# A two-layer hybrid encoder layer on one core: projections 512 columns wide, channel-major gates, x fed transposed, transposes issued singly, one weight ring

## The chip, the cores and the metric

The kernel runs on one core of a Trainium2 chip. Its time is the device time of one execution in microseconds (us). The core has five engines that this text names as the profile does: PE (TensorE, matmuls and transposes, with PEld for its weight loads), DVE (VectorE), ACT (ScalarE), POOL (GpSimd) and SP (SyncE), which here only issues the transfers between HBM and the on-chip memory, one after the other, each after the semaphores that it waits for.

## What is computed

One layer over 2048 positions of width 1024, in float32. The input is RMS-normalised and projected to 4616 columns; three groups of heads read the projection; their outputs are joined, projected back and added to the input.

```python
h = rms_norm(x, norm_g[l])
proj = jnp.einsum('bsd,de->bse', h, w_in[l])
(a_q, a_k, a_v, a_z, m_q, m_k, m_v, m_o, m_z, m_i, m_f, c_a, c_b, c_z) = split_columns(proj)
...
att = chunk_band_attention(q, k, v, ...) * jax.nn.silu(a_z)      # 4 heads of 64, own chunk + 8 before
qk = jax.nn.silu(causal_depthwise_conv(concat([m_q, m_k]), ...)) # width 4
hm = mlstm_chunkwise(m_q, m_k, m_v, i_pre, f_pre)                # 4 heads of 128
ml = rms_norm(sigmoid(m_o) * hm, ml_out_g) * jax.nn.silu(m_z)
u = causal_depthwise_conv(c_a * jax.nn.sigmoid(c_b), ...)        # width 31
cv = jax.nn.silu(layer_norm(u, ...)) * jax.nn.silu(c_z)
x = x + jnp.einsum('bse,ed->bsd', concat([att, ml, cv]), w_out[l])
```

## The kernel before

The sequence is worked through in four rounds of 512 positions (`q` in the code, `TQ` = 512), each of four blocks of 128. In each round x is loaded row by row (`x_load`), scaled by its RMS, transposed on PE in tiles of 128x128 and split into two parts, high and low, of the rounded type `fp32r`, so that three matmul passes (high x high, high x low, low x high: `PASS`) stand for one float32 matmul. The two halves of a round's transposed x are the tiles `xT` of 256 positions each.

The projection is cut into 21 units of 256 columns (264 for the one that carries the gates), and the output projection into 4 of them. A unit is computed in one of two ways. `tm` gives positions on the partitions: for a block of 128 positions 8 k-steps of 3 passes, 24 matmuls with a moving operand of 256 weight columns. `cm` gives channels on the partitions: 128 channels, and twice 24 matmuls that move 256 positions each. Keys, queries, values, the gates o and z of each mLSTM head, the gate of the convolution group and the output are `tm`; the inputs of both convolutions and the attention gate are `cm`.

Weights arrive in the first round as float32 (`fetch_w`, tiles `wr`), are split by ACT (high part) and POOL (low part) in `split_w`, are written back to HBM split (`keep`, `wk<-w`) and are loaded split in the later three rounds (`fetch_split`, `w<-wk`). Two pools hold them: 6 tiles `wr`, 10 tiles `w`.

PE's order is the order in which the code calls it. A clock in the code (`clk`, advanced by an assumed price of each matmul) and coroutines (`spawn`, `tick`, `wait_for`) place the work of the attention, the mLSTM heads and the layer norm between the k-steps of the units: a coroutine yields a time from the table `L`, and its next piece is put on PE when the code's clock has passed it. So a transpose or a matmul of a head that needs a result of DVE stands a fixed piece of PE's work behind it; if the result is later than that, PE, which works in order, waits. For head h `do_head` computes the unit with k and q (`cm` twice); `conv_silu` takes each result off PSUM (ACT copy to `mraw`, then on DVE one scaling and three multiply-adds into `macc`, a tanh on ACT, one last multiply on DVE). `head_chain` then transposes k (`pk`), `L["kk"]` = 8.52 after k's unit, multiplies k by q (`pS`), `L["qq"]` = 8.0 after q's unit, and goes through the four blocks (`pp`, three matmuls each). The width-31 convolution is 60 multiply-adds a round on DVE (`cvu`), fed in one by one (`TAP`). The other engines and SP are ordered by the framework's scheduler.

Of the kernel before, what the change touches and what calls it, by code (L numbers as in the profile page):

```python
# [26 lines left out]
U_AK, U_AV, U_AQ, U_AZ, U_CZ = 0, 1, 2, 3, 4  # L27
U_V = (5, 6)
U_QK = (7, 8, 9, 10)
U_OZ = (11, 12, 13, 14)  # L30
U_C = (15, 16)
WB = 10
RB = 6
XB, OB, HB = 6, 6, 6
PTB, QSB, PRB = 2, 1, 3
DEPTH = 3
TAP = 2.21
LNH = 3
L = {"x": 6.51, "xg": 1.4, "k": 11.25, "q": 5.7, "qt": 1.48, "s": 0.32, "t": 1.6, "pv": 0.45, "s0": 4.0,
     "g0": 14.0, "g1": 4.37, "g2": 6.03, "g3": 5.23, "g4": 2.6, "kk": 8.52, "qq": 8.0, "ps": 2.2, "ch": 2.4,  # L40
     "ln": 3.61, "mix": 0.79, "wp": 1.85, "w0": 0.19, "xb": 0.5, "mx1": 1.12, "mx2": 1.39}
U_OUT = (17, 18, 19, 20)
# [3 lines left out]
def kernel(ctx: ExitStack, tc: tile.TileContext, x, wu, wg, norm_g, qg, kg, bias, far,  # L46
# [7 lines left out]
    xpool = ctx.enter_context(tc.tile_pool(name="xpool", bufs=3))  # L54
# [14 lines left out]
    def slot(name, n, dt=F32, tag="H"):  # L69
        return sl.tile([P, n], dt, name=name, tag=tag, bufs={"X": XB, "O": OB, "H": HB}[tag],  # L70
                       padded_shape=[P, 512 if tag == "X" else 516])
# [7 lines left out]
    gx = ctile([P, D], "gx")  # L79
    mask = ctile([P, P], "mask")  # L80
    G.memset(mask, 0.0)
    G.affine_select(out=mask, in_=mask, compare_op=ALU.is_ge, fill=NEG, base=0,
                    pattern=[[1, P]], channel_multiplier=-1)
    mhalf = ctile([P, 16], "mhalf")
    G.memset(mhalf, -0.5)
    zrow = ctile([16, P], "zrow")
    G.memset(zrow, 0.0)

# [7 lines left out]
    mlg = ctile([P, 512], "mlg")  # L96
    cvw_t = ctile([P, 2, CW], "cvw_t")
    cvb_t = ctile([P, 2], "cvb_t")
    lng = ctile([P, 256], "lng")
    lnb = ctile([P, 256], "lnb")  # L100
    wgs = ctile([P, 2, KT, 8], "wgs", F32R)
    wgr = ctile([P, KT, 8], "wgr")

    def load_consts():
        nc.sync.dma_start(out=gqk, in_=qg.partition_broadcast(P))
        nc.sync.dma_start(out=kg_t, in_=kg.partition_broadcast(P))
        V.scalar_tensor_tensor(out=gqk, in0=gqk, scalar=0.125, in1=kg_t, op0=ALU.mult, op1=ALU.mult)
        nc.sync.dma_start(out=bias_t, in_=bias.rearrange("h p k -> p h k"))
        nc.sync.dma_start(out=far_t, in_=far.partition_broadcast(P))
        G.memset(bias_t[0:64, :, 192:256], NEG)  # L110
        nc.sync.dma_start(out=mcw_t, in_=mcw)
# [19 lines left out]
    cvh = ctile([P, 2, CW - 1], "cvh")  # L131
    for h in range(4):
        G.memset(cst[h], 0.0)
    G.memset(mst, 0.0)
    G.memset(mch, 0.0)
    G.memset(cvh, 0.0)

# [854 lines left out]
```

## Time and profile before

| | |
|---|---|
| time, median of 3 runs | 1252.62 us (1251.28 to 1252.7) |
| profiled execution: its time, and its span | 1250.82 us, 1249.0 us |
| busy share of the span: PE, DVE, ACT, POOL | 96%, 65%, 31%, 21% |
| mean granted TensorE clock | 0.996 of full |
| moved by the DMA engines | 235.51 MB, mean 189 GB/s |

The span runs from the first to the last instruction of the profiled execution; what lies around it is 1.8 us. The profile prints busy times, which for PE count a matmul from its start to its modelled end while the next one already runs; so the distance between starts, not the printed mean of one matmul, is what a matmul costs.

### The profile page before, as it was taken

What the parts mean: (1) busy time and instruction counts of PE and PEld (TensorE: products, weight loads), DVE (VectorE), ACT (ScalarE), POOL (GpSimd) and SP (SyncE); (2) the same over time, 40 slices, a digit from 0 to 9 for tenths busy, and PEclk for the clock granted to TensorE, in tenths of its full rate; (3) what the DMA queues carried; (4) which work ended last, traced back from release to release, by engine and by line L of the source; (5) the groups of instructions that cost most, each with busy time, mean ns of one, the idle gap of its engine ahead of it and who ended that gap; (6) DMA issues with size and microseconds to landing.
All of it is one profiled execution on the core that took longest, in us unless ns stands there. A gap on an engine that the chain in (4) does not pass through costs nothing.

```text
span 1249.0 us, 25880 instructions
## 1 busy us (share of the span) xinstructions
PE 1201.4 (96%) x10188; PEld 1177.1 (94%) x10188; DVE 815.0 (65%) x2125; ACT 390.2 (31%) x1023; POOL 262.1 (21%) x312
## 2 busy tenths in 40 slices
PE   6999989889899999999999999999999999999998
PEld 6999889889899999999999999999999999999998
DVE  7368998884316888876431788877632288887641
ACT  5345433333122442223221343222312144322220
POOL 5553444644111000130010100013101010012200
PEclk9999999999899999999999999999999999999999
DMA  9956465668745244454675432555476532345453
GB/s 315 366 205 218 164 226 203 220 220 281 266 167 197 88 134 152 152 189 181 239 238 185 163 110 85 184 189 186 151 248 244 203 138 86 135 162 184 162 179 127
DMA packets 101345, 235.51 MB, mean 189 GB/s; under 512 B 11560, under 2 KB 45160, under 8 KB 101224
## 3 DMA queue, kind: packets, MB, share of 16 engines
q1 hardware_dynamic: 101224, 233.87, 54.2%
q8 instruction: 80, 1.31, 0.4%
q14 instruction: 41, 0.34, 0.1%
HBM read 181.27 MB, written 52.56 MB: 187 GB/s over the span
## 4 chain that ended last, share of the span: by engine, by line
PE 79%; DVE 10%; DMA 5%; issue 3%; POOL 2%; ACT 1%; SPq 0%; POOLq 0%; ACTq 0%; DVEq 0%
PE pmm L155 64%; PE pp L155 3%; PE pss L155 2%; PE po L155 2%; PE ptp L160 2%; DMA dt<-fr 2%; PE ptx L160 2%; DVE macc L634 1%; DMA wk<-w 1%; DVE cvu L726 1%; PE pS L155 1%; POOL w L248 1%; DMA wr<-in_wu 1%; PE ptq L160 1%; DVE dt L648 1%
## 5 line engine op out<-in xcount | busy, mean ns | idle before, releaser
L155 PE MATMUL pmm<-w,xT 128*128 128x256 f32 (+1 forms) x3840 | 516.5, 287 | 6.7 <-DVE xT L266 2.4
L155 PEld LDWEIGHTS pmm<-w,xT 128*128 128x128 f32 x3840 | 476.5, 190 | 12.0 <-issue 2.9
L155 PE MATMUL pmm<-xT,w 128*128 128x256 f32 x2688 | 344.6, 285 | 0.0
L155 PEld LDWEIGHTS pmm<-xT,w 128*128 128x128 f32 x2688 | 327.7, 189 | 2.3 <-issue 1.9
L155 PE MATMUL pmm<-w,mT 128*128 128x256 f32 x1536 | 198.0, 286 | 8.1 <-DVE xr L914 6.5
L155 PEld LDWEIGHTS pmm<-w,mT 128*128 128x128 f32 x1536 | 187.8, 191 | 9.6 <-DVE xr L914 6.9
L726 DVE SCALAR_TENSOR_TENSOR cvu<-cvu,cvw_t 128x512 f32<-128x512 f32 x240 | 184.3, 768 | 0.9
L248 POOL TENSOR_TENSOR w<-wr,w 128x512 fp32r<-128x512 f32 x80 | 110.9, 1397 | 117.6 <-ACT w L208 104.1
L621 POOL TENSOR_TENSOR gz<-gz,mlg 128x512 f32<-128x512 f32 x16 | 23.8, 1486 | 326.0 <-DVE gz L618 266.1
L914 DVE TENSOR_TENSOR xr<-pmm,xr 128x256 f32<-128x256 f32 x64 | 27.0, 423 | 91.8 <-PE pmm L155 75.3
L634 DVE SCALAR_TENSOR_TENSOR macc<-mraw,mcw_t,macc 128x512 f32<-128x512 f32 x96 | 75.6, 787 | 1.0
L720 DVE SCALAR_TENSOR_TENSOR cvu<-cvt,pmm 128x512 f32<-128x512 f32 x8 | 5.5, 690 | 102.5 <-PE pmm L155 102.5
L208 ACT ACTIVATE pr<-pr,nm 128x640 f32<-128x640 f32 (+4 forms) x64 | 49.1, 767 | 45.1 <-DVE nm L463 45.0
L208 ACT CAST w<-wr 128x512 fp32r<-128x512 f32 x82 | 49.2, 616 | 8.2 <-issue 4.0
L208 ACT ACTIVATE kw<-og 128x128 f32<-128x128 f32 x64 | 19.8, 310 | 99.3 <-DVE og L689 91.9
L208 ACT CAST xT<-ptx 128x512 fp32r<-128x512 f32 x32 | 18.8, 587 | 99.8 <-PE ptx L160 99.7
L208 ACT COPY pT<-ptp 128x384 f32<-128x384 f32 (+2 forms) x64 | 29.5, 461 | 59.3 <-PE ptp L160 59.3
L155 PE MATMUL pss<-kT,qT 128*128 128x320 f32 (+4 forms) x224 | 44.6, 315 | 2.8 <-DVE nm L463 2.8
L681 DVE SCALAR_TENSOR_TENSOR cst<-cst,dec,pp 128x129 f32<-128x129 f32 x64 | 22.2, 348 | 33.9 <-PE pp L155 33.5
L208 ACT ACTIVATE og<-pmm 128x128 f32<-128x128 f32 x64 | 17.5, 274 | 81.8 <-PE pmm L155 81.7
L160 PE MATMUL ptp<-ident_r,pr 128*128 128x128 f32 x280 | 41.8, 273 | 0.0
L155 PE MATMUL po<-pT,vR 128*64 128x128 f32 x560 | 38.9, 279 | 0.6 <-DVE pT L487 0.5
(251 smaller groups left out, 1384.3 us busy)
## 6 DMA issues: line engine op xcount, KB each, us to landing
w<-wk SPq DMA_DIRECT2D x240, 512.0 KB, 5.2
wk<-w SPq DMA_DIRECT2D x80, 512.0 KB, 5.3
wr<-in_wu SPq DMA_DIRECT2D x84, 256.0 KB, 4.7
xs<-in_x SPq DMA_DIRECT2D x16, 512.0 KB, 6.2
xr<-in_x SPq DMA_DIRECT2D x64, 128.0 KB, 2.7
out<-xr SPq DMA_DIRECT2D x64, 128.0 KB, 4.6
w<-wk SPq DMA_DIRECT2D x12, 528.0 KB, 5.5
dt<-fr SPq DMA_DIRECT2D x16, 256.0 KB, 3.3
```

The source lines that it names most:

```text
L155: last[0] = tc.keep_in_program_order(PE.matmul(out_, lhsT=lhsT, rhs=rhs, start=start, stop=stop))
L160: tc.keep_in_program_order(PE.transpose(out=out_, in_=in_, identity=(ident_r if rnd else ident)[0:n, 0:n]))
L208: i = fn(*a, **k)
L248: lo = G.tensor_tensor(out=w[:, 1, :, 0:256], in0=raws[g], in1=f(w[:, 0, :, 0:256]), op=ALU.subtract)
L621: G.tensor_tensor(out=gz, in0=gz, in1=mlg[:, h * P:(h + 1) * P].unsqueeze(1).to_broadcast([P, NB, P]), op=ALU.mult)
L634: V.scalar_tensor_tensor(out=acc, in0=raw[:, j:j + 512], scalar=mcw_t[:, i, j:j + 1], in1=acc, op0=ALU.mult, op1=ALU.add)
L648: V.scalar_tensor_tensor(out=dt[:, b, :], in0=dt[:, b, :], scalar=cols[:, 0, h, b:b + 1], in1=mask, op0=ALU.add, op1=ALU.min)
L681: V.scalar_tensor_tensor(out=cst[h], in0=cst[h], scalar=dec[:, h * NB + b:h * NB + b + 1], in1=pu[:, 0:129], op0=ALU.mult, op1=ALU.add)
L720: V.scalar_tensor_tensor(out=u[:, CW - 1:CW + 511], in0=t, scalar=1.0, in1=pa, op0=ALU.add, op1=ALU.mult)
L726: queue_after(V.scalar_tensor_tensor(out=acc, in0=u[:, i:i + 512], scalar=cvw_t[:, j, i:i + 1], in1=acc, op0=ALU.mult, op1=ALU.add), last[0])
L914: V.tensor_tensor(out=xr, in0=ps[:, 0:256], in1=xr, op=ALU.add)
```

## The change

- Every unit is 512 wide. `tm` now moves 512 weight columns (k and v of the attention in one unit, all of m_v, all of m_o), `cm` moves all 512 positions of the round. The query unit with the gates stays at 264.
- The gates z of the mLSTM heads, the gate of the convolution group and the output projection are computed with channels on the partitions (`cm`). The norms of the heads' outputs (`og`, scaled on ACT) and of the convolution group are transposed after normalising (`pto`, `pty`) and gated there; the per-channel factors (`mlg`, `lng`, `lnb`) become per-partition scalars. The output is written transposed, and turned on the host.
- x is also passed in transposed (`xT` in HBM), and x's transposes on PE go. The rows of x are still read for the sums of squares; the row factors reach the transposed x by a matmul of ones with a diagonal (`spread`, `prs`). `x_first` does this for the first round block by block, `x_next` for a later round during the output projection.
- In a coroutine `yield FINE` puts each transpose behind one matmul (`sip`), where four stood together.
- One ring of 12 tiles (`WB`) holds both unsplit weights (two pieces in a tile) and split ones. Weights are handled in 84 pieces; a `tm` unit uses 8 of them (4 for the queries) in each block and frees them in the last, a `cm` unit uses 2.
- `conv_silu`: the scaling is done by ACT from PSUM, the small copies by POOL; there is one buffer for `mraw` (tag "M") and two for `macc` (tag "A", shared with x's tiles `xk`), where both came from a pool of 6. A head's units are put on PE only after the head before has taken its q (`"taken"`).
- The order of the units and the constants `L`, `TAP` are new.

```diff
-WB = 10
-RB = 6
-XB, OB, HB = 6, 6, 6
+WB = 12
+LAG = 5
+XB, HB, AB, MB = 5, 4, 2, 1
...
-     "g0": 14.0, "g1": 4.37, "g2": 6.03, "g3": 5.23, "g4": 2.6, "kk": 8.52, "qq": 8.0, "ps": 2.2, "ch": 2.4,
+     "g0": 15.0, "g1": 4.8, "g2": 6.0, "g3": 5.7, "g4": 2.8, "kk": 9.3, "qq": 8.8, "ps": 2.4, "ch": 2.6,
...
+FIRST = ["kv", "cb0", "ca0", "cb1", "ca1", "qg", "v", "mk0", "mq0", "o"]
+LATER = ["cb0", "ca0", "kv", "cb1", "ca1", "qg", "v", "mk0", "mq0", "o"]
...
-        clk["t"] += max(n, 256) / 2400.0 if lhsT.dtype == F32R else 4.0 * n / 2400.0
+        clk["t"] += 0.006 + 0.00044 * n if lhsT.dtype == F32R else share * 2 * (0.003 + n / 1200.0)
...
+    def sip():
+        for c in chains:
+            if c["fine"]:
+                step(c)
+                return
...
+    def new_w(i, j):
+        flat = wpool.tile([P, 1056], F32R, name=f"w_{i}", tag="w", bufs=WB)
+        ring.append(lambda: j < st["used"] and (j >= NPIECE or i in kept))
+        return flat[:, 0:2 * cols(i)].rearrange("p (a c) -> p a c", a=2)
...
+    def keep(i, w):
+        kept[i] = dram.tile([P, 2, cols(i)], F32R, name=f"wk_{i}", tag=f"wk_{i}")
+        nc.sync.dma_start(out=f(kept[i]), in_=f(w))
...
-    def tm(xts, wt, b, n=256):
-        for k in range(KT):
-            for s_, m_ in PASS:
-                mm(ps[:, 0:n], xt[:, s_, k, c], wt[k // 2][:, m_, k % 2, 0:n], i == 0, i == 3 * KT - 1)
+    def tm(xt, u, b):
+        for k in range(KT):
+            w = piece((st["used"] if b == NB - 1 else j0 + k // step_))
+            for s_, m_ in PASS:
+                mm(ps[:, 0:n], xt[:, s_, k, c], w[:, m_, :], i == 0, i == 3 * KT - 1)
+                sip()
...
-    def cm(xts, wt, c0):
-        for p in range(2):
-            for k in range(KT):
-                for s_, m_ in PASS:
-                    mm(ps[:, p * 256:(p + 1) * 256], wt[k // 2][:, s_, k % 2, c0:c0 + P], xts[p][:, m_, k, :],
-                       i == 0, i == 3 * KT - 1)
+    def cm(xt, u):
+        for k in range(KT):
+            w = piece(st["used"]).rearrange("p a (k c) -> p a k c", k=4)
+            for s_, m_ in PASS:
+                mm(ps, w[:, s_, k % 4, :], xt[:, m_, k, :], i == 0, i == 3 * KT - 1)
+                sip()
...
+    def x_first(xt):
+        for b in range(NB):
+            t = io.tile([P, D], F32, name="xs", tag="io", padded_shape=[P, 1056])
+            nc.sync.dma_start(out=t, in_=x[b * P:(b + 1) * P, :])
+            xtb = raw[:, b * D:(b + 1) * D].rearrange("p (k t) -> p k t", k=KT)
+            nc.sync.dma_start(out=xtb, in_=xT[:, b * P:(b + 1) * P].rearrange("(k p) t -> p k t", p=P))
...
+            dg = spread(rs, [b])
+            mm(pr[:, 0, :], ones, dg[:, 0, :], True, True)
...
+    def x_next(q, xt, lnc):
+        while not lnc["done"]:
+            yield 0.5
...
+        for k in range(KT):
+            xk = slot("xk", 512, tag="A")
+            nc.sync.dma_start(out=xk, in_=xT[k * P:(k + 1) * P, q * TQ:(q + 1) * TQ])
+            if k:
+                finish_x(xt, k - 1, prev, rb)
...
-    def conv_silu(q, ps, i):
-        raw = slot("mraw", 516)
-        V.tensor_copy(out=raw[:, 0:3], in_=mch[:, i, :])
+    def conv_silu(ps, i):
+        raw = slot("mraw", 516, tag="M")
+        G.tensor_copy(out=raw[:, 0:3], in_=mch[:, i, :])
         A.copy(out=raw[:, 3:515], in_=ps)
-        acc = slot("macc", 512)
-        V.tensor_scalar(out=acc, in0=raw[:, 3:515], scalar1=mcw_t[:, i, 3:4], scalar2=mcb_t[:, i:i + 1],
-                        op0=ALU.mult, op1=ALU.add)
+        acc = slot("macc", 512, tag="A")
+        A.activation(out=acc, in_=ps, func=AF.Identity, scale=mcw_t[:, i, 3:4], bias=mcb_t[:, i:i + 1])
...
+    def do_head(q, xt, h, vt, gc, cols, dec, FR, before):
+        hb["c"] = spawn(head_chain(q, h, hb, vt, gc, cols, dec, FR, before))
+        if before:
+            wait_for(lambda: "taken" in before)
+        hb["k2"] = conv_silu(cm(xt, f"mk{h}"), 4 + h)
+        hb["q2"] = conv_silu(cm(xt, f"mq{h}"), h)
...
-        for u in range(4):
-                ps = tm(mts, wt, b)
-                V.tensor_tensor(out=xr, in0=ps[:, 0:256], in1=xr, op=ALU.add)
-                nc.sync.dma_start(out=out[q * TQ + b * P:q * TQ + (b + 1) * P, u * 256:(u + 1) * 256], in_=xr)
+        for i in range(KT):
+            ps = cm(mt, f"out{i}")
+            V.tensor_tensor(out=xr, in0=ps, in1=xr, op=ALU.add)
+            nc.sync.dma_start(out=out[i * P:(i + 1) * P, q * TQ:(q + 1) * TQ], in_=xr)
```

Where the instructions stand is decided by the coroutines and the scheduler. On SP, at the very start, the transfers stood so before (`xs` are rows of x, `wr` unsplit weights, `gx` the norm's factor):

```order
L285 DMA xs<-in_x 128x1024
L287 DMA gx<-in_norm_g 128x1024
L285 DMA xs<-in_x 128x1024
L221 DMA wr_0_159<-in_wu 128x512
L221 DMA wr_1_161<-in_wu 128x512
L221 DMA wr_2_163<-in_wu 128x512
L221 DMA wr_3_165<-in_wu 128x512
L285 DMA xs_1_179<-in_x 128x1024 x2
```

Now the rows of x for the second block are the 38th transfer (`rw` are unsplit weights, `wk` the stores of split ones, `xraw` the transposed x); these are the transfers ahead of it, with the first block's rows the first of all:

```order
L295 DMA rw_201<-in_wp 128x512 x2
L301 DMA wk_204<-w_191 128x1024
L301 DMA wk_206<-w_196 128x1024
L125 DMA far_t<-in_far 128x4
L127 DMA gb_t<-in_gb 128x8
L128 DMA mcw_t<-in_mcw 128x32
L129 DMA mcb_t<-in_mcb 128x8
L130 DMA mlg<-in_ml_g 128x4
L132 DMA lng<-in_ln_g 128x2
L133 DMA lnb<-in_ln_b 128x2
L419 DMA xs<-in_x 128x1024
```

All four loads of the first round's rows stood within the first nine; now the second to fourth stand behind all eight stores of the first unit's split weights (each of which waits for its split) and behind the constants.

On PE, the third mLSTM head of the second round stood so before, from within the unit that follows its q unit (whose last matmul is 18 matmuls further up) to `pS`:

```order
L155 MATMUL pmm_6918<-w_6730,xT_0_3898 128x256 x6
L155 MATMUL pmm_6947<-w_6574,xT_0_3898 128x256 x6
L155 MATMUL pmm_6947<-w_6576,xT_0_3898 128x256 x3
L160 MATMUL pk<-ident_r,macc 128x128 x4
L160 MATMUL ptl<-ident_r,cvu 128x128 x2
L155 MATMUL pmm_6947<-w_6576,xT_0_3898 128x256 x3
L155 MATMUL pmm_6947<-w_6728,xT_0_3898 128x256 x6
L155 MATMUL pmm_6947<-w_6730,xT_0_3898 128x256 x6
L155 MATMUL pmm_6998<-w_6574,xT_1_4305 128x256 x6
L155 MATMUL pmm_6998<-w_6576,xT_1_4305 128x256 x6
L155 MATMUL pmm_6998<-w_6728,xT_1_4305 128x256 x6
L155 MATMUL pS<-macc 128x128 x4
```

The same head now, from the end of its q unit to `pS` (`pp` belong to the head before, `z` is the gate of the second head):

```order
L171 MATMUL pmm_mq_4966<-xT_2813,w_4486 128x512 x3
L171 MATMUL pp<-vt,kw 128x129
L171 MATMUL pp<-vt,dt 128x129
L171 MATMUL pp<-cst_116,iw 128x129
L171 MATMUL pmm_mq_4966<-xT_2813,w_4486 128x512 x3
L171 MATMUL pmm_mq_4966<-xT_2813,w_4492 128x512 x12
L176 MATMUL pk<-ident_r,macc 128x128 x4
L171 MATMUL pmm_z_5051<-xT_2813,w_4497 128x512 x12
L171 MATMUL pmm_z_5051<-xT_2813,w_4502 128x512 x12
L171 MATMUL pS<-macc 128x128 x4
```

`pk` now stands at once behind the q unit and `pS` one unit of 24 wide matmuls further, where 66 narrow ones stood between the q unit and `pS`.

## Rows read from the trace of the kernel before

**Rows 1.** The page, part 1: busy us, share of the span, instructions of each engine.
```profile
PE 1201.4 (96%) x10188; PEld 1177.1 (94%) x10188; DVE 815.0 (65%) x2125; ACT 390.2 (31%) x1023; POOL 262.1 (21%) x312
```
**Rows 2.** Windows, one for each round: length, busy us by engine, PEclk, DMA share, GB/s.
```profile
0.00:339.10 339.10, 302.48 (x2466) 293.10 (x2466) 239.90 (x531) 133.11 (x333) 157.01 (x162) 0.98 0.69 243
339.10:641.70 302.60, 300.39 (x2589) 295.84 (x2587) 194.49 (x537) 88.64 (x235) 36.13 (x53) 1.00 0.51 173
641.70:946.40 304.70, 301.65 (x2589) 296.04 (x2586) 195.42 (x537) 88.20 (x235) 35.99 (x53) 1.00 0.51 174
946.40:1249.00 302.60, 296.90 (x2555) 292.15 (x2553) 185.16 (x521) 80.23 (x220) 32.92 (x44) 1.00 0.46 159
```
**Rows 3.** Groups of PE's instructions by form: count, busy us, mean ns, idle before.
```profile
L155 PE MATMUL pmm<-w,xT 128*128 128x256 f32 x3456 | 463.5, 287 | 5.4 <-DVE xT L266 2.4 <-DVE gz L618 2.0 <-DVE w L242 0.6
L155 PE MATMUL pmm<-xT,w 128*128 128x256 f32 x2688 | 344.6, 285 | 0.0
L155 PE MATMUL pmm<-w,mT 128*128 128x256 f32 x1536 | 198.0, 286 | 8.1 <-DVE xr L914 6.5 <-DVE mT L266 1.6
...
L160 PE MATMUL ptx<-ident_r,xs 128*128 128x128 f32 x128 | 21.1, 293 | 7.7 <-DVE xs L307 7.4 <-issue 0.3
```
**Rows 4.** The chain that ended last, a gapless stretch: start us, us, what.
```profile
364.18 31.53 PE pmm L155 x264
```
**Rows 5.** The same chain in a short stretch: a pair of 512-wide matmuls.
```profile
128.19 0.47 PE pss L155 x2
```
**Rows 6.** Timeline of PE at 128 us: the 512-wide pair and what follows.
```profile
128.03 0.63 PE L155 MATMUL pss<-kT,qT 128*128 128x512 f32 x2
128.49 0.28 PE L155 MATMUL pmm<-w,xT 128*128 128x256 f32 x1
```
**Rows 7.** The chain again: four transposes together, and one alone.
```profile
299.94 0.44 PE ptx L160 x4
...
93.46 0.11 PE ptp L160
```
**Rows 8.** Groups of PE's instructions in the first 40 us.
```profile
L155 PE MATMUL pmm<-w,xT 128*128 128x256 f32 x159 | 24.7, 311 | 3.4 <-DVE xT L266 2.4 <-DVE w L242 0.6 <-ACT w L208 0.3
L160 PE MATMUL ptx<-ident_r,xs 128*128 128x128 f32 x32 | 6.7, 355 | 7.7 <-DVE xs L307 7.4 <-issue 0.3
```
**Rows 9.** The start: issues on SP's queue, from the timeline (start us, us).
```profile
4.11 1.12 SPq L285 DMA_DIRECT2D xs<-in_x  x2
...
8.66 0.33 SPq L105 DMA_DIRECT2D gqk<-in_qg  x1
...
14.72 0.33 SPq L114 DMA_DIRECT2D mlg<-in_ml_g  x1
```
**Rows 10.** The chain at the start: what a transfer takes from issue to landing.
```profile
7.68 7.03 DMA wr<-in_wu
```
**Rows 11.** A window over the middle of the first round.
```profile
70.00:300.00 230.00, 210.39 (x1755) 202.68 (x1754) 193.08 (x449) 95.92 (x261) 110.44 (x97) 1.00 0.61 209
```
**Rows 12.** Groups of DVE's instructions: count, busy us, mean ns, idle before.
```profile
L695 DVE SCALAR_TENSOR_TENSOR og<-og,mrs,gz 128x128 f32<-128x128 f32 x64 | 22.9, 419 | 6.4 <-POOL mrs L273 6.1
...
L631 DVE TENSOR_SCALAR macc<-mraw,mcw_t,mcb_t 128x512 f32<-128x512 f32 x32 | 19.9, 620 | 0.0
L618 DVE SCALAR_TENSOR_TENSOR gz<-tz,pmm 128x128 f32<-128x128 f32 x64 | 17.8, 279 | 3.1 <-ACT tz L208 2.5
```
**Rows 13.** Timeline, one convolution of the second round: first and last step.
```profile
526.95 0.59 ACT L208 COPY mraw<-pmm 128x512 f32<-128x512 f32 x1 [1.72 <-PE pmm L155]
...
532.44 0.69 DVE L637 SCALAR_TENSOR_TENSOR macc<-mraw,macc 128x512 f32<-128x512 f32 x1 [0.76 <-ACT mraw L208]
```
**Rows 14.** Timeline, one convolution of the first round: first and last step.
```profile
174.84 0.59 ACT L208 COPY mraw<-pmm 128x512 f32<-128x512 f32 x1 [1.35 <-PE pmm L155]
...
186.49 0.68 DVE L637 SCALAR_TENSOR_TENSOR macc<-mraw,macc 128x512 f32<-128x512 f32 x1
```
**Rows 15.** PE's waits: who for whom, us in total, times, longest.
```profile
PE pk L160 <- DVE macc L637: 5.5, 3, 2.8
```

More of the change, by code (lines that the diff above doesn't have):

```diff
@@ new lines, in bank_wait, with cols, ring_free @@
+    def bank_wait():
+        while not bank_free():
+            yield 0.2
+    order = [(q, u) for q in range(NQ) for u in order_of(q)]
+    seq = [(q, u, i) for q, u in order for i in PIECES[u]]
+    kept = {}
+    ready = {}
+    st = {"raw": 0, "split": 0, "load": NPIECE, "used": 0, "at": 0}
+    raws = {}
+    late = []
+    box = {}
+    def cols(i):
+        return 528 if i in GATED else 512
+    ring = []
+    def ring_free():
+        return len(ring) < WB or ring[-WB]()
+    def new_w(i, j):
+        flat = wpool.tile([P, 1056], F32R, name=f"w_{i}", tag="w", bufs=WB)
+        ring.append(lambda: j < st["used"] and (j >= NPIECE or i in kept))
+        return flat[:, 0:2 * cols(i)].rearrange("p (a c) -> p a c", a=2)
@@ new lines, in raw_fetch @@
+    def raw_fetch():
+        while st["raw"] < min(NPIECE, st["split"] + LAG) and ring_free():
+            j = st["raw"]
+            flat = wpool.tile([P, 1056], F32, name=f"rw_{j}", tag="w", bufs=WB)
+            ring.append(lambda: st["split"] > j + 1)
+            for a in range(2):
+                i = seq[j + a][2]
+                raw = flat[:, a * 528:a * 528 + cols(i)]
+                nc.sync.dma_start(out=raw, in_=wq[i - PIECES["qg"][0]] if i in GATED else wp[i])
+                raws[j + a] = raw
+            st["raw"] += 2
@@ new lines, in load_pieces, with spent, next_unit @@
+    def load_pieces():
+        while st["load"] < len(seq) and st["split"] == NPIECE and not late and ring_free():
+            j = st["load"]
+            i = seq[j][2]
+            w = new_w(i, j)
+            nc.sync.dma_start(out=f(w), in_=f(kept[i]))
+            ready[j] = w
+            st["load"] += 1
+    def spent(n=1):
+        for _ in range(n):
+            ready.pop(st["used"])
+            st["used"] += 1
+        load_pieces()
+    def next_unit(name):
+        q, u = order[st["at"]]
+        assert u == name, (u, name)
+        st["at"] += 1
+        return u
@@ L638, in conv_silu, with head_chain @@
         return acc
[L640 to L641 removed]
+    def head_chain(q, h, hb, vt, gc, cols, dec, FR, before):
+        while not gc["done"] or before and "free" not in before:
             yield 0.5
@@ new lines, in head_chain @@
+        hb["want"] = True
+        while ("z", h) not in box:
+            yield 0.5
+        yield 1.5
+        yield from bank_wait()
+        pt, pt_ = bank("pto")
+        for b in range(NB):
+            tp(pt[:, b, :], og[:, b, hs])
+            yield FINE
+        gz = box.pop(("z", h))
+        V.scalar_tensor_tensor(out=gz, in0=pt.rearrange("p a b -> p (a b)"), scalar=mlg[:, h:h + 1], in1=gz,
+                               op0=ALU.mult, op1=ALU.mult)
+        shut(pt_)
+        split_to(mixed(), 4 + h, gz)
@@ L888 @@
[L888 to L896 removed]
+            split_to(mixed(), g, ao[:, g, :])
+        zgate(3)
+        if q + 1 < NQ:
+            nxt = xtile(f"xT_{q + 1}")
+            spawn(x_next(q + 1, nxt, lnc))
+        wait_for(lambda: lnc["done"] and all(hb["c"]["done"] for hb in heads))
```

846 lines of the change are left out of this document (415 added, 431 removed).

## The prediction

> **What bounds the kernel now.** The page's busy shares come first: PE 96% of the span, DVE 65%, the others less [rows 1]. A busy share of PE says little by itself, so the stages come next. A window over each round [rows 2] shows three later rounds of 302.6 to 304.7 us in which PE is idle for 2.2 us in the second, 3.1 in the third and 5.7 in the last (length less PE's busy time), and a first round of 339.1 us with 36.6 us idle. So rounds two to four are as long as PE's own work, and are shortened only by less of it; the first round also waits. The groups by form [rows 3] then say what PE's work is: 3456 + 2688 + 1536 = 7680 projection matmuls of 256 columns (384 more are 264 wide and stay so). In a gapless stretch of the chain 264 matmuls take 31.53 us [rows 4], 119.4 ns each. 7680 of them are 917 us of the 1249.
>
> **The width.** The order of the changed kernel has 3840 matmuls of 512 columns in their place. Their price stands in the trace: the attention's score matmuls are 512 wide in a few places. One pair starts at 128.03, and the next matmul starts at 128.49 [rows 6]: 0.46 us for two, 230 ns each. The chain gives the same pair 0.47 us, 235 ns [rows 5]. So two narrow matmuls, 238.8 ns, become one of 230: the columns set the price, not the number of instructions. 3840 x 8.8 ns = 34 us less; by the chain's price 3840 x 3.8 = 15. I take **-34**, because the distance between starts is the direct measurement, with -15 and, if a long run of wide ones comes out 5 ns better than this pair, -53 as ends.
>
> The Trainium skill ("TensorE: Matmul & The Clock Gate", Back-to-back issue gap) gives N/2.4 + 2.5 ns between warm matmuls, so 109.2 and 215.8 ns, and a gain of 2.6 ns a pair, -10 us in place of -34. The trace has more at both widths (119.4 and 230), so its rows decide. The same section names some 131 ns for a sustained stream of 512-wide matmuls, which would take 417 us off; no wide matmul in this trace is near it.
>
> **Transposes.** x's 128 transposes on PE, 32 of them in the first 40 us [rows 8], go: four cost 0.44 us [rows 7], so -14.1. The row factors add 16 float32 matmuls of ones, each two instructions; at 0.11 us each, the nearest row, 32 x 0.11 = +3.5. Issuing transposes singly moves nothing for the float32 ones, since one alone costs 0.11 us, as much as a quarter of four [rows 7]. For the 192 transposes of rounded q and k no single one is in the trace; if each costs what a lone float32 one does in place of some 0.09, that is +3.5, and nothing at the other end. Together **-7** (-11 to -7).
>
> **The start.** In the first 40 us PE gets through 159 matmuls at 0.119, 32 transposes at 0.11 and little else [rows 8], 23 us of work: 17 us are lost, waiting for transfers of 6 to 7 us [rows 10] and for x's scaling. Before, all rows of x were issued by 5.2 us [rows 9]. Now block two's rows stand behind 37 transfers, among them eight stores, each of which waits for a split of the first unit's weights by ACT, DVE or POOL. My estimate: the last weight pieces land at about 16 us (issued near 9, 7.03 in flight [rows 10]), are split by some 20, SP then passes seven constants, of which eight took from 8.66 to 14.72 [rows 9], so the rows of block two are issued at about 26 and land at 32; squares, scaling and splitting them takes some 4 us more. PE has done block one (24 x 0.23 = 5.5 us) by then and starts block two at about 36: 30 us lost in place of 17. I take **+14**; the ends are 0 (the stores find their splits early) and +20.
>
> **The middle of the first round.** From 70 to 300 us PE is idle for 230.0 - 210.4 = 19.6 us while DVE is busy for 193.1, 84% [rows 11]: DVE is late there. The change takes work off DVE: the convolutions' scaling goes to ACT (19.9 us over four rounds), the gating of the heads by rows (22.9 + 17.8) [rows 12] becomes 32 wide operations of about 0.69 (the mean of L637's [rows 13]), 22 us. That is about 10 us less for DVE in each round.
>
> **The heads.** What works the other way is the distance that PE's order leaves to a convolution. Priced by the rows above, the old order had 81 narrow matmuls (9.6 us) between a k unit and `pk`, and 66 with a few transposes (8.5 us) between a q unit and `pS`. The new order has, for the second to fourth heads, 6.8 to 9.4 us to `pk`, and to `pS` 6.8, 4.6 and 2.7 us in the first round, 8.3, 5.9 and 5.5 in the second, 11.1, 5.2 and 2.9 in the last two. A convolution takes, from ACT's copy to DVE's last step, 526.95 to 533.13 = 6.2 us in the second round [rows 13], and 174.84 to 187.17 = 12.3 in the first [rows 14]; the old distance nearly always covered the former, and PE's waits at `pk` are 5.5 us in all [rows 15]. So PE will now wait at `pS` where the distance is under about 6.3: round two 0.4 and 0.8, rounds three and four 1.1 and 3.4 each. With `pk` and the single `mraw` buffer, for which q's copy waits until k's convolution is through, I round to **+10** for rounds two to four (+2, if the lighter DVE brings the chain to 5 us; +45, if it is 10). In the first round, at a chain of 10 us after DVE's relief, a head waits 3 to 8 us: some 15, in place of the 19.6: **-5** (-20 to +10). Behind a waiting `pS` on PE stand the next unit, and with it the `pp` of the head before.
>
> **The turns and the end.** At the end of the first round PE waited 5.9 us once for a load of x and 8.1 in all at the output [rows 3]. Now x's squares are summed before and during the output projection, and its eight k-steps follow on DVE and ACT, two buffers deep, while PE still has 96 wide matmuls (22 us). I take **-4** for the first turn (-8 to +4) and **+3** for the other two and a last output transfer twice as large (0 to +20). Weights: 84 pieces of 512 KB a round as before, so no term.
>
> **Sum.** -34 - 7 + 14 + 10 - 5 - 4 + 3 = -23. The profiled execution took 1250.8 us, span 1249.0; with the change about 1228, span 1226. The runs' median is 1.8 above that execution, so I predict **1229.5 us**.
>
> **Rivals.**
> 1. *The waits do not come* (chance 0.20). DVE's relief shortens the convolutions to about 5 us, which covers most distances, and the first round's lag goes: heads +2, first round -15, the rest as above: -41, 1211 us; with an early start 1200. For it: DVE has 10 us less a round. Against it: rounds two to four shrink by as much, so DVE's share stays.
> 2. *The heads become the bound; slower* (0.12). Place: `pS` of the third and fourth heads, rounds two to four. If the chain there is 10 us and not 6.3, each of nine heads (three in each round) waits 4 us more: +36, 1266 us. It decides from a chain of about 8.9 us on, where the 23 us to the old time are used up. For it: 12.3 us were seen in the first round; one buffer in place of a pool of six. Against it: 6.2 in a later round.
> 3. *x is late at every turn* (0.10). If a step of `xk` takes a transfer plus DVE and ACT, two deep, 8 steps need 28 us against the 22 that PE has left: +6 at each of three turns, 1247 us.
> 4. *Width buys almost nothing* (0.05). At the chain's 235 ns the term is -15: 1249 us. The Trainium skill's gap formula, named above, would come out there too.
> 5. *A long run of wide matmuls is cheaper than the pair* (0.03): at 225 ns, 1210 us. The skill's sustained figure would be far beyond; the 230 of this trace speaks against it.
>
> **Chances.** My forecast, 1213 to 1243, has 0.50; its own spread comes from the start (14), the heads (10) and the first round. The range has to reach to rival 1 on one side and to half of rival 2 on the other: **1198 to 1256**. A measurement of this kernel tells 0.2%, 2.5 us, from no change: faster means under 1250.1, slower over 1255.1. Faster: 0.50 + 0.20 + 0.03 + most of rivals 3 and 4, less the forecast's own tail: 0.80. Slower: rival 2 and a little of 3 and 4: 0.14. Same: 0.06.
>
> **What the profile after would show.** The width: a long stretch of 512-wide matmuls in the chain at about 230 ns each. The start: PE's first block done by 20 us and its second unit-block starting near 36, with SP's load of x behind the stores. The heads: PE's waits at `pS` for the last step of `macc`, of 1 to 4 us each, some 10 us over rounds two to four. The lighter DVE: under 800 us of busy time. The turns: PE waiting for the next `xT` by no more than a few us. I am wrong if waits at `pS` or for x are several times that, if wide matmuls stand at another price, or if the ring of weights, to which I gave no term, makes PE wait for pieces.

## The result: 2.6% slower, and the profile after

| | before | after |
|---|---|---|
| time, median of 4 runs each | 1252.66 us | 1286.76 us |
| ratio, 95% interval | | 1.0264 (1.0233 to 1.0295) |
| profiled span | 1249.0 us | 1286.3 us |

The forecast was 1229.5 us with a range of 1198 to 1256, so it was wrong in sign and by 57 us. The page after, part 1, answers to [rows 1]:

```profile
PE 1188.2 (92%) x6252; PEld 962.2 (75%) x6252; DVE 766.2 (60%) x1849; ACT 434.2 (34%) x984; POOL 243.3 (19%) x325
```

PE has 13 us less busy time and its share fell from 96 to 92%. The four rounds after, as [rows 2] (length, then busy us of PE, PEld, DVE, ACT, POOL, then PEclk, DMA share, GB/s):

```profile
0.00:345.50 345.50, 296.28 (x1457) 236.43 (x1458) 220.37 (x456) 144.53 (x323) 151.59 (x166) 0.95 0.70 250
345.50:659.00 313.50, 296.39 (x1602) 241.51 (x1600) 185.75 (x471) 100.92 (x228) 30.47 (x55) 0.99 0.52 173
659.00:972.70 313.70, 298.19 (x1602) 241.99 (x1602) 184.07 (x467) 99.45 (x226) 31.69 (x55) 0.99 0.52 175
972.70:1286.30 313.60, 297.38 (x1593) 242.28 (x1593) 176.04 (x455) 89.33 (x207) 29.54 (x49) 0.98 0.45 150
```

Idle time of PE (length less busy) is 49.2, 17.1, 15.5 and 16.2 us, where it was 36.6, 2.2, 3.1 and 5.7: 50 us more in all. The later rounds, which were as long as PE's own work before, now wait. Two rows of the chain that ended last show that the price of a wide matmul is not the reason (start us, us, what):

```profile
300.55 5.56 PE pmm_out L171 x24
...
365.53 17.96 PE pmm_kv L171 x78
```

That is 231.7 and 230.3 ns for each, the price that the prediction took from [rows 6]. Two things have to be explained: the 50 us of waiting, and why PE's busy time fell by only 13 us where the forecast took 41 off it (width and transposes).

A large part of the second is the clock. In nine stretches of the profile after, which hold or follow waits of PE, the granted clock is 0.50, the lower of its two levels (1.2 GHz). One of them, and the sum over the nine (columns as above):

```profile
235.30:242.10 6.80, 5.88 (x18) 5.01 (x19) 4.44 (x8) 3.03 (x8) 1.78 (x4) 0.50 0.42 127
sum 61.60, PE 43.37 PEld 34.06 DVE 31.20 ACT 15.44 POOL 11.80; mean PE 4.82 PEld 3.79 DVE 3.47 ACT 1.72 POOL 1.31
```

PE is busy for 43.4 us at that level, and was for 8.1 us before. At 427 ns for a wide matmul in place of 230 (last section) this is an estimated 16 us more than before, for which the prediction has no term. PE's waits (who for whom, us in total, times, longest):

```profile
PE prs L171 <- ACT dg L233: 24.8, 3, 15.2
PE pS L171 <- DVE macc L775: 19.0, 9, 3.7
...
PE pmm_cb L171 <- ACT xT L233: 6.3, 3, 5.4
PE pss L171 <- DVE nm L605: 6.2, 4, 2.6
PE ptp L176 <- ACT qT L233: 4.3, 3, 1.6
PE pss L171 <- ACT qT L233: 4.1, 1, 4.1
...
PE pmm_out L171 <- DVE xr L1020: 3.3, 2, 2.4
PE ptl L176 <- DVE kw L799: 2.7, 3, 0.9
```

There are four places: the start (`prs`, the row factors), the heads (`pS`), the attention's transposes and scores (`ptp` for the probabilities, with `ptq` and `ptk` for q and k further down; `pss` are the scores), and the turns between rounds (`pmm_out`, `pmm_cb`: the output's units and the next round's first one). `ptl` is a transpose of the layer norm.

**The start.** PE's timeline (start us, us, what, in brackets the idle time before it), and SP's queue:

```profile
12.65 7.24 PE L171 MATMUL pmm_kv<-w,xT 128*128 128x512 f32 x22 [1.69 <-DVE xT L446]
35.12 0.80 PE L171 MATMUL prs<-dg,ones 128*128 128x128 f32 x2 [15.23 <-ACT dg L233]
37.80 1.22 PE L171 MATMUL pmm_kv<-w,xT 128*128 128x512 f32 x2 [1.88 <-ACT xT L233]
```
```profile
27.81 0.33 SPq L133 DMA_DIRECT2D lnb<-in_ln_b  x1
29.05 0.33 SPq L419 DMA_DIRECT2D xs<-in_x  x1
```

Block two's rows are issued at 29.05 us behind stores and constants, and the block starts at 37.8 (forecast: 26 and 36). In the first 75 us PE is idle for 31.2 us, where it was for 11.1.

**The first turn.** DVE's steps on `xk` (the first column is the start):

```profile
324.91 1.42 DVE L493 SCALAR_TENSOR_TENSOR xk<-xk,gx,rb 128x512 f32<-128x512 f32 x2 [1.51 <-ACT rb L233]
...
336.37 1.44 DVE L493 SCALAR_TENSOR_TENSOR xk<-xk,gx,rb 128x512 f32<-128x512 f32 x2 [1.08 <-DMA xk<-in_xT]
...
346.32 1.41 DVE L493 SCALAR_TENSOR_TENSOR xk<-xk,gx,rb 128x512 f32<-128x512 f32 x2
...
353.88 1.42 DVE L493 SCALAR_TENSOR_TENSOR xk<-xk,gx,rb 128x512 f32<-128x512 f32 x2 [4.78 <-DMA xk<-in_xT]
355.32 1.36 DVE L399 TENSOR_TENSOR xT<-xk,xT 128x512 fp32r<-128x512 f32 x2
```

Two steps go at a time, for two buffers, some 10 us from pair to pair, so the eight take 32 us, from 324.9 to the last split's end at 356.7. PE has 22 us of the output projection there and then 18 matmuls of the next unit, 4 us, before it needs the last two steps. Between the pairs stands the transfer, from issue to landing in the chain:

```profile
328.26 8.02 DMA xk<-in_xT
...
339.21 6.80 DMA xk<-in_xT
```

**The heads.** The third head's q convolution in the third round (copy, last step, and the product that needs it):

```profile
855.30 0.59 ACT L233 COPY mraw<-pmm_mq 128x512 f32<-128x512 f32 x1 [2.01 <-PE pmm_mq L171]
...
862.03 0.69 DVE L775 SCALAR_TENSOR_TENSOR macc<-mraw,macc 128x512 f32<-128x512 f32 x1
...
862.77 1.59 PE L171 MATMUL pS<-macc 128*128 128x128 f32 x8 [2.36 <-DVE macc L775]
```

It is 7.4 us from the copy to the end of the last step, and the product starts with it: the distance in PE's order was too short by 2.4 us.

### The profile page after: what moved, and what is told of

Same layout as the page of the kernel before. It is cut to its first block, busy times and chain, and to the rows that moved or that the text cites. A ratio compares the mean times of both kernels' runs of the same rounds, so it can differ in the third digit from the quotient of the medians.

```text
span 1286.3 us, 17454 instructions
## 1 busy us (share of the span) xinstructions
PE 1188.2 (92%) x6252; PEld 962.2 (75%) x6252; DVE 766.2 (60%) x1849; ACT 434.2 (34%) x984; POOL 243.3 (19%) x325
## 4 chain that ended last, share of the span: by engine, by line
PE 65%; DMA 13%; DVE 12%; ACT 3%; POOL 3%; issue 2%; SPq 1%; ACTq 0%; DVEq 0%; POOLq 0%
PE pmm_o L171 7%; PE pmm_out L171 7%; PE pmm_v L171 6%; PE pmm_kv L171 6%; PE pmm_z L171 5%; PE pmm_mk L171 4%; DMA xk<-in_xT 4%; PE pmm_ca L171 4%; PE pmm_az L171 3%; PE pmm_qg L171 3%; PE pp L171 3%; PE pmm_mq L171 3%; PE pmm_cz L171 3%; PE pmm_cb L171 3%; DMA dt<-fr 3%; DMA out<-xr 2%
## 5 line engine op out<-in xcount | busy, mean ns | idle before, releaser
L171 PE MATMUL pmm_out<-mT,w 128*128 128x512 f32 x768 | 181.0, 395 | 3.3 <-DVE xr L1020 3.3
L171 PEld LDWEIGHTS pmm_out<-mT,w 128*128 128x128 f32 x768 | 143.8, 188 | 35.4 <-DVE xr L1020 4.1
L320 POOL TENSOR_TENSOR w<-rw,w 128x512 fp32r<-128x512 f32 (+1 forms) x76 | 106.0, 1407 | 91.3 <-ACT w L233 82.6
L171 PE MATMUL pmm_mk<-xT,w 128*128 128x512 f32 x384 | 114.7, 431 | 0.0
L171 PE MATMUL pmm_v<-w,xT 128*128 128x512 f32 x384 | 109.2, 420 | 0.0
L171 PE MATMUL pmm_o<-w,xT 128*128 128x512 f32 x384 | 106.6, 418 | 0.0
L171 PE MATMUL pmm_mq<-xT,w 128*128 128x512 f32 x384 | 106.2, 412 | 0.0
L171 PE MATMUL pmm_kv<-w,xT 128*128 128x512 f32 x384 | 99.3, 416 | 6.4 <-ACT xT L233 3.9
L171 PE MATMUL pmm_z<-xT,w 128*128 128x512 f32 x384 | 102.8, 416 | 0.0
L171 PEld LDWEIGHTS pmm_kv<-w,xT 128*128 128x128 f32 x384 | 75.6, 200 | 26.8 <-ACT xT L233 5.0
L171 PEld LDWEIGHTS pmm_mq<-xT,w 128*128 128x128 f32 x384 | 69.1, 189 | 15.5 <-issue 1.0
```

Of the source, the lines that this page charges most:

```text
L171: last[0] = tc.keep_in_program_order(PE.matmul(out_, lhsT=lhsT, rhs=rhs, start=start, stop=stop))
L320: lo = G.tensor_tensor(out=w[:, 1], in0=raw, in1=f(w[:, 0]), op=ALU.subtract)
```

## The experiments

Ratios are to the kernel before, with 95% intervals. The first four change one thing each in the changed kernel; gains are differences of medians, against 1286.76 us.

**x's loads first.** Two tiles take the rows of blocks three and four, so that all loads can be issued at once.

```diff
+        two = io.tile([P, 2, D], F32, name="xs", tag="og", bufs=1)
         for b in range(NB):
-            t = io.tile([P, D], F32, name="xs", tag="io", padded_shape=[P, 1056])
+            t = two[:, b - 2] if b > 1 else io.tile([P, D], F32, name="xs", tag="io", padded_shape=[P, 1056])
             nc.sync.dma_start(out=t, in_=x[b * P:(b + 1) * P, :])
...
             xb.append(xtb)
+        for b in range(NB):
+            t, xtb = xs[b], xb[b]
```

> All four blocks of x (rows and transposed) are loaded before the first weight store and the constants; nothing else moves. If the loss at the start is x standing behind stores and constants on SP (41 us lost by 75 us in the changed kernel, against 17 in the kernel before), PE's second block starts near 20 us in place of 37.8 and the time falls by 18 to 24 us, to about 1263 to 1269. Rival: the first unit's weights, now behind 4 MB of x in the transfers, become the late ones; then the gain is under 6 us, 1281 or more.

Measured: 1271.69 us, 1.0158 (1.0129 to 1.0187), 15 us less than the changed kernel. PE's timeline:

```profile
20.91 0.50 PE L171 MATMUL pmm_kv<-w,xT 128*128 128x512 f32 x1 [2.11 <-ACT w L233]
...
25.58 0.80 PE L171 MATMUL prs<-dg,ones 128*128 128x128 f32 x2 [0.41 <-ACT dg L233]
27.81 6.27 PE L171 MATMUL pmm_kv<-w,xT 128*128 128x512 f32 x18 [1.43 <-ACT xT L233]
```

The second block starts 10 us earlier, not 18: the rival's part is seen at 20.91, where the last weights of the unit are now late. The order of SP's queue, with the two tiles that another order needs, is the cause of 15 us.

**The attention gate's units ahead of the convolution gate's.**

```diff
         head(3)
-        wait_for(lambda: box.pop("ln", False))
-        for j in range(2):
-            box["cz", j] = gate(cm(xt, f"cz{j}"), "cz")
-        zgate(2)
         wait_for(lambda: att["done"])
-        for g in range(2):
+        for g in (0,):
             t = gate(cm(xt, f"az{g}"), "az")
...
+        wait_for(lambda: box.pop("ln", False))
+        box["cz", 0] = gate(cm(xt, "cz0"), "cz")
+        box["cz", 1] = gate(cm(xt, "cz1"), "cz")
+        zgate(2)
         zgate(3)
```

The list of units (`PLAN`) is put in the same order, so that the weights come in it.

> Only the place of two units of PE's order: the attention gate's two units stand before the convolution gate's two, where they stood behind them. First theory, the order itself: where the code must wait for a coroutine to finish before it may put the next unit on PE, it moves its clock forward with no work in between, and PE then waits for real; in the changed kernel these jumps sum to 68.2 us (17.4 in the first round's heads and norm, 9 to 13 in each later one, and 4.5 a round before the output), and this edit takes out the 24.6 us of them that stand at the layer norm, so the time falls by 15 to 25 us, to 1262 to 1272. Second theory, late convolutions through one buffer each: only the fourth head's waits at its k-times-q product go (10.5 us in the four rounds), 1276 to 1280, and the third head's stay as they are.

Measured: 1269.54 us, 1.0134 (1.0103 to 1.0165), 17 us less. PE's wait at the product, to be read against 19.0 above:

```profile
PE pS L169 <- DVE macc L773: 9.3, 5, 3.7
```

There are five waits in place of nine, 9.7 us less, and the waits at `ptl` (2.7 us) are gone. The size is the first theory's, the place mostly the second's: the fourth head's four waits are gone, and the third head's stay. The run with grouped transposes, below, speaks against the jumps of the code's clock as the measure: there they sum to 11 us more and the time is 18 us less.

**Every wide matmul as two narrow ones.**

```diff
+        for p in range(2):
+            h = slice(p * 256, p * 256 + 256)
+            i = 0
             for k in range(KT):
...
-                    mm(ps, w[:, s_, k % 4, :], xt[:, m_, k, :], i == 0, i == 3 * KT - 1)
+                    mm(ps[:, h], w[:, s_, k % 4, :], xt[:, m_, k, h], i == 0, i == 3 * KT - 1, half=True)
```

> Each 512-wide projection matmul is done as two of 256, half a unit after the other; weights, transfers, order of units and the code's clock stay. If width is worth what the prediction took (230 ns for 512, 119.4 for 256, 3840 pairs), PE's work grows by 34 us, and the waits, which are behind dependencies and not filled by it, stay or shrink a little: 1308 to 1322. Rival: the gain of width was never there because it only lengthened waits: within 8 us of 1287.

Measured: 1292.49 us, 1.0328 (1.0297 to 1.0358): only 6 us more than with wide ones. In this kernel the width is worth next to nothing; either it has no price, or what it saves is waited away. The pair further down tells these apart. The edit brings one thing along: a coroutine may step after every third narrow matmul, so about twice as often.

**Transposes in groups again**, every `yield FINE` taken out:

```diff
         for h in range(4):
             tp(pt[:, h, :], stk[:, h, :])
-            yield FINE
```

> Transposes go to PE in groups again, not one behind each matmul; nothing else is changed. If a single rounded transpose costs some 30 ns more behind a wide matmul than in a group (350 against 321 ns for the pair), 192 of them are worth 6 us and the time falls to 1280 to 1284. Rival: a coroutine that issues its group at once comes to its next step at another time of the code's clock, whose jumps sum to 79 us in place of 68, and the time rises by some 5 to 11 us.

Measured: 1269.00 us, 1.0142 (1.0112 to 1.0172), 18 us less: three times the first theory's figure, against the second one's sign. All waits of `ptp`, and the 4.1 us of `pss` for `qT`, are gone from the list; those of `pS` rise from 19.0 to 23.3 us, as the places of what follows move too. What one of the waits was is seen in the changed kernel's timeline of PE at 458 us, and in ACT's:

```profile
458.07 0.22 PE L176 MATMUL ptq<-ident_r,qstk 128*128 128x128 f32 x1
458.13 0.45 PE L171 MATMUL pmm_mq<-xT,w 128*128 128x512 f32 x1
458.42 0.22 PE L176 MATMUL ptq<-ident_r,qstk 128*128 128x128 f32 x1
...
459.10 0.22 PE L176 MATMUL ptq<-ident_r,qstk 128*128 128x128 f32 x1
...
462.63 0.33 PE L176 MATMUL ptp<-ident_r,pr 128*128 128x128 f32 x1 [1.57 <-ACT qT L233]
```
```profile
461.47 0.63 ACT L233 ACTIVATE mraw<-macc 128x512 f32<-128x512 f32 x1 [2.48 <-DVE macc L772]
462.01 0.57 ACT L233 CAST qT<-ptq 128x512 fp32r<-128x512 f32 x1
```

Four transposes that would have stood together (73 ns from start to start in the grouped run) take from 458.07 to 459.10. There are two PSUM banks for transposes. By the time the bank is full, ACT already stands at the tanh of a convolution, for which it waits 2.48 us; the copy that empties the bank comes behind it, and PE, which needs a bank for `ptp`, waits 1.57.

One wide matmul with one transpose takes 0.35 us, 0.12 more than alone. Counted over undisturbed places of the trace at the upper clock, from one wide matmul to the second one behind the last transpose and less 231 ns for each wide matmul, a transpose of q or k costs 114 ns singly and 92 to 93 in groups, and a float32 one 111 to 114 against some 110. For the 192 and the 472 of them that is an estimated 5 us over the kernel on PE itself. In the two profiled executions, 20 us apart, PE's busy time is 10.2 us less with groups (1178.0 against 1188.2) and its idle time 10.1 us less. The part of the 10.2 that is not the transposes' own price goes with the clock: 43 wide matmuls stand some 427 ns from the next with groups, 69 in the changed kernel, which is 5 us.

That the held bank is what lies behind all of the waits that went was not tested apart, with a third bank for example.

**The three edits together**, then with coroutines allowed a step behind every wide matmul, and the same with narrow matmuls; and buffers.

> The three edits that each helped by themselves, together: x's loads first, the attention gate's units ahead of the convolution gate's, transposes in groups. If their gains of 15, 17 and 18 us are of different waits they add up: 1286.8 - 50 = about 1237. If they took out the same waits, the sum is less: 1250 to 1258. The code's clock still jumps by 54 us in all.

Measured: 1238.98 us, 0.9894 (0.9869 to 0.9919). The three gains add up (50 expected, 48 measured), so the edits take out different waits.

```diff
                 i += 1
                 sip()
+                if i % 3:
+                    tick()
```

> As the three edits together, and a coroutine may also step behind every wide matmul, not only behind every third. It is the wide half of a pair that differs in width alone; the code's clock jumps by 51 us in place of 54. Expected: within 4 us of the three edits together.

Measured: 1245.50 us, 0.9948 (0.9933 to 0.9964), 6.5 us more than without the finer steps; the cause stays open.

> As the wide half of the pair, with each projection matmul done as two of 256 columns; steps of coroutines stand 0.36 us of PE's work apart and the code's clock jumps by 52 us. In the changed kernel itself narrow matmuls cost only 6 us, because they filled waits. If the width is worth 8 to 9 ns a pair wherever PE does not wait, taking waits away must bring the term out: 15 to 30 us above the wide half. If the width is worth little by itself, within 8 us of it.

Measured: 1277.77 us, 1.0206 (1.0185 to 1.0227). Narrow matmuls cost 32.3 us here, 8.4 ns a pair; PE's busy time is 27.5 us more (1206.4 against 1178.9). The steps of the two are near each other but not the same (0.36 and 0.23 us of PE's work apart), and against the run without the finer steps the difference is 38.8 us. So with the waits reduced the width is worth about what the prediction said, 34 us; in the changed kernel most of it was waited away.

```diff
-WB = 12
-XB, HB, AB, MB = 5, 4, 2, 1
+WB = 11
+XB, HB, AB, MB = 5, 4, 3, 2
```

> The changed kernel with two buffers for the convolutions' raw input and three for their sums, paid for by a weight ring of 11 tiles in place of 12. If the waits at the k-times-q product (15.1 us in rounds two to four, 7.1 in the first) come from q's copy waiting for the one buffer, they fall by half or more and the time by 8 to 15 us, to 1272 to 1279. If they come from the order, which leaves PE too little between q's unit and the product, nothing much moves: 1283 to 1291. A ring one tile shorter could cost some us of waits for weights at the units that hold 8 pieces; these would show at the first matmuls of such units.

Measured: 1264.42 us, 1.0101 (1.0072 to 1.0129), 22 us less than the changed kernel, but not for the first reason given:

```profile
PE pS L171 <- DVE macc L775: 18.5, 9, 3.8
```

It is 18.5 us against 19.0: the second raw buffer does nothing for the product. The theory of the one buffer falls. PE's waits for `xT` before the later rounds' first unit (`pmm_cb` for ACT, 6.3 us) were gone, which points to the third buffer of `xk`.

**Only the buffers of `xk` and of the sums** (`AB` = 4, `MB` = 1, `WB` = 11):

> The changed kernel with one buffer for the convolutions' raw input as before, four for sums and x's steps, and a weight ring of 11. It splits the gain of 22 us that two raw buffers, three sum buffers and a ring of 11 gave together. If x's steps at the turns are the place (in the changed kernel they go two at a time, 10 us a pair, because there are two buffers), the turns' waits of 11.5 us before the first unit fall under 3 and the time is 1262 to 1268 again. If it was the second raw buffer, the time is 1280 or more.

Measured: 1265.72 us, 1.0112 (1.0097 to 1.0127), 21 us less. DVE at the first turn, and the round that follows:

```profile
318.57 2.74 DVE L493 SCALAR_TENSOR_TENSOR xk<-xk,gx,rb 128x512 f32<-128x512 f32 x4 [1.53 <-ACT rb L233]
...
335.12 0.74 DVE L493 SCALAR_TENSOR_TENSOR xk<-xk,gx,rb 128x512 f32<-128x512 f32 x1
335.79 1.47 DVE L399 TENSOR_TENSOR xT<-xk,xT 128x512 fp32r<-128x512 f32 x2
```
```profile
339.30:641.00 301.70, 293.00 (x1602) 239.87 (x1601) 182.37 (x467) 99.70 (x226) 30.49 (x55) 1.00 0.54 181
```

The first four of the eight steps now go at once, all take 18.7 us in place of 32, and the second round is 301.7 us long in place of 313.5. No wait of `pmm_cb` is left. That is 11.8 of the 21 us. Of the rest, 6.2 us lie in the first round, where PE's 4.1 us at `pss` for `qT` are gone and its waits at `prs` are 3.0 us less; whether the buffers or the ring of 11 did that stays open.

**Only the attention's transposes in groups**: `yield FINE` taken out behind the transposes of `pr` and `qstk` alone.

> Only the attention's transposes (probabilities, and rounded queries) go to PE in groups; all others stay single. If single transposes cost time because a half-filled bank of transposes (there are two) is held for as long as three to five wide matmuls, and the attention, with 472 of the transposes, waits for a bank again and again, this alone gives most of the 18 us that grouping all gave: 1268 to 1274. If the loss lies in the heads' and the norm's transposes, 1280 or more.

Measured: 1275.57 us, 1.0192 (1.0175 to 1.0208): 11 of the 18 us, between the two expectations. The attention has the larger part, the other chains the rest.

**Everything together**: the three edits and the four buffers.

> The three edits together (1239 us) with four buffers for sums and x's steps and a ring of 11. The waits before the first unit of rounds two to four (9.4, 3.1 and 1.1 us with the three edits) should fall under 3 in all: 1227 to 1231. If the first round or the units with 8 pieces wait for weights in the shorter ring, 1235 or more.

Measured: 1227.90 us, 0.9825 (0.9796 to 0.9854), faster than both kernels. On top of the three edits the buffers gave 11.1 us (1238.98 to 1227.90), not the 21 that they gave alone: with the three edits in, PE's waits at `pmm_cb` were 11.6 us in all, and other waits, such as the 4.1 us of `pss`, the edits had taken out already. The second to fourth rounds:

```profile
326.80:624.90 298.10, 291.62 (x1602) 241.70 (x1601) 181.99 (x467) 100.43 (x226) 28.40 (x55) 1.00 0.54 182
624.90:924.10 299.20, 292.34 (x1602) 241.69 (x1601) 182.24 (x467) 100.17 (x226) 28.38 (x55) 1.00 0.54 184
924.10:1225.00 300.90, 291.07 (x1594) 240.72 (x1592) 172.25 (x451) 89.08 (x205) 26.52 (x49) 1.00 0.46 154
```

PE is still idle for 6.5 to 9.8 us in each. The two largest waits left over the whole execution are these; 5.3 us of the first lie in the later rounds, and none of the second:

```profile
PE pS L169 <- DVE macc L772: 12.8, 8, 3.8
PE prs L169 <- ACT dg L231: 9.7, 3, 6.9
```

**The best version with single transposes.**

> The best version so far (1227.9 us) with its transposes issued one by one again, as the changed kernel does. If single transposes hold the two transpose banks and so delay the attention whatever else waits, the time rises by 12 to 18 us, to 1240 to 1246, with waits at the attention's transposes and scores. If they only hurt through waits that the other three edits have taken away, it stays within 4 us of 1228.

Measured: 1239.25 us, 0.9904 (0.9869 to 0.9939), 11 us more than in groups. Waits of `ptp` are back:

```profile
PE ptp L174 <- ACT qT L231: 2.8, 3, 1.4
...
PE ptp L174 <- ACT pT L231: 1.7, 3, 0.6
```

So single issue costs by itself, not only through the waits that the other edits took out. In the two profiled executions PE's busy time is 8.4 us more (1180.0 against 1171.6), some 5 of it the transposes' own price as worked out above, and its idle time 4.0 us more.

## Why the prediction was wrong

The step that failed is the one under the whole sum: that what PE's work loses comes off the time, with 18 us of new waits against it, since the later rounds were "as long as PE's own work". The sum took 41 us off PE's work and gave 18 back. Measured, PE's busy time fell by 13 us and its idle time grew by 50. Of the 28 us that are missing in the busy time, an estimated 16 are the lower clock after waits, which the sum puts at nothing without a word, some 7 the width (27.5 us in the pair that differs in it, not 34), and 1 or 2 the single transposes. Of the 50 us of idle time the start has 20, where the sum had 14; the rest of the first round has 8 less than before; and rounds two to four have 38, where the sum had 10 for the heads and 3 for the turns and the end. By the lists of waits of those rounds the heads have 12 of the 38, the turns 11 (`pmm_cb` and `pmm_out`: 12.6 us, before 1.3), and the attention's scores and transposes, with small transposes that use the same banks, some 12 (13.8 us, before 1.3). Term by term:

- **The width, -34: near in size, not in effect.** It is 230 to 232 ns a wide matmul in the chain, and 32.3 us in the pair of kernels that differ in it. But the working took PE's work off the time at once. That holds only while PE is the bound; in the changed kernel it was not, and 6 us were left.
- **"Issuing transposes singly moves nothing" failed.** The step priced the instruction on PE and put at most +3.5 on it. That price was about right (an estimated 5 us), but single issue measured 18 us in the changed kernel and 11 in the best one. The step forgot the resource that a transpose holds: a bank takes four to five times as long to fill (1.03 us from the first start to the last, where a group takes 0.22), there are two, and the copy that empties it falls behind other work on ACT. No rival named it.
- **The turns, "-4" and "+3": failed.** The working saw "two buffers deep" and 22 us of PE's work, and rival 3 had the mechanism, with 28 us for the eight steps, a wait at all three turns and a chance of 0.10. At the first turn they took 32 us: two transfers of the chain took 8.0 and 6.8 us from issue to landing while the DMA engines were busy for 98% of the time from 300 to 345 us. That turn has 5.4 of the 6.3 us that PE waited for `xT` there; at the two others it waited for 0.5 each. More buffers gave 21 us back in the changed kernel, 11.8 of them in the round after the first turn, and 11 on top of the other edits.
- **The start, +14: right place, too small.** Block two started at 37.8 us (forecast 36), but the row factors of the fourth block kept PE waiting for another 2.6 us, and after 15 us without work PE ran at the lower clock (last section). PE is idle for 20 us more than before in the first 75 us. Loading x first gave 15 us back, and left waits for weights and x in their place.
- **The heads, +10: right.** The waits at `pS` for the convolution in rounds two to four are 12.4 us in 6 waits, at the third and fourth heads, with chains of 6.0 to 8.4 us in those places. The prediction's suspicion of the one raw buffer was wrong: q's copy starts 0.1 us after its unit's end there, and a second buffer left the waits at 18.5 of 19.0 us. Moving two units of PE's order took out half of them, with the waits at `ptl`: 17 us in time, of which the list of waits shows 12.
- **The first round's middle, -5: hardly seen.** The lighter DVE came (766 us, forecast under 800), but waits at `pS`, `pss` and `pp` took the place of the old ones: PE is idle for 18.0 us from 70 to 300 us, where it was for 19.6. The first round is 6.4 us longer.
- **The rivals.** Rival 2 had the sign and place, not the size: the chain was not 10 us. The slower side came from three places together, the start, the transposes and the turns, and from the clock after their waits; each had been given too little or nothing. With x loaded first, two units moved, transposes grouped and more buffers for `xk`, the time was 1227.9 us, 2 us from the forecast. That is luck and not the forecast come true: it is another kernel, and in it PE is busy for 11 us more than the sum had and idle for 12 us less.

Two numbers ahead of the result are off without bearing on it. The projection has 4360 columns, not 4616; with the output's 4 units its 17 make the 21. And the 417 us that the prediction works out from a figure of 131 ns are 414 (3840 x 107.8 ns).

What stays open: what the shorter ring did in the runs with more buffers, why finer steps of the coroutines cost 6.5 us, whether narrow matmuls profited in the changed kernel from the finer steps that they bring along, and how much of the price of single transposes is the held bank.

## What to carry to other kernels

In this kernel a cheaper instruction on the engine that is 96% busy was worth its price only where what feeds the engine kept up: the same width was worth 6 us in one version and some 32 in another. When PE's work in a stage shrinks by 10 us, list each chain that was hidden behind it and what room it had. Price not only an instruction but what it holds: a transpose here holds a PSUM bank until another engine copies it out, and two buffers with a transfer of 7 to 8 us let two steps through in 10 us. Price a wait with the clock behind it: the same matmul took 427 in place of 230 ns after some waits. An order that is written out by hand with a clock in the code needs the same care as a price: the order on SP (15 us) and two units moved on PE (17 us) together made as much as the width.

## What the runs showed of the hardware that was not expected

After some of its waits PE did not come back at its speed. PE's timeline after the 5.4 us wait at the first turn, and windows there (PEclk is the third value from the end):

```profile
356.66 1.91 PE L171 MATMUL pmm_cb<-xT,w 128*128 128x512 f32 x4
358.37 3.19 PE L171 MATMUL pmm_ca<-xT,w 128*128 128x512 f32 x7
```
```profile
350.00:355.00 5.00, 0.00 (x0) 0.00 (x0) 1.12 (x2) 0.33 (x1) 0.00 (x0) 0.97 0.66 208
...
358.00:360.00 2.00, 2.00 (x6) 1.59 (x5) 0.00 (x0) 0.60 (x1) 0.00 (x0) 0.50 0.23 33
```

At a granted clock of 0.50, the lower of its two levels (1.2 GHz), four wide matmuls take from 356.66 to 358.37, 427 ns each, against 230 at the upper. In the trace 11 matmuls from 356.66 on stand some 427 ns apart before the distance is 235 again, so 2.2 us are paid on top of this wait; after the long wait of the start eight stand so from 40.4 us on. Counted over the whole trace 69 wide matmuls do, eight of them in the first 17 us; that is 13.6 us more than at 230 ns. In the version with all four edits it is 43. The nine stretches at 0.50 each hold or directly follow a wait of 1.9 to 15.2 us; other waits of that size, such as 2.4 us for `xr` before 652.39 us, have none. The Trainium skill ("TensorE: Matmul & The Clock Gate", Back-to-back issue gap) gives N/1.2 for the lower level, 427 ns, and there the trace agrees; its 215.8 for the upper one is below the 230 measured.
